# VectorE in traced order through the down-projection and final norm, with the row sums added on GpSimd

## The chip, the core and the metric

The kernel runs on one core of one Trainium2 chip. A core has five engines, each with an instruction queue of its own that it works through in order: TensorE (PE, matmuls; its weight loads are shown as PEld), VectorE (DVE), ScalarE (ACT), GpSimd (POOL) and SyncE (SP, which here only issues DMA transfers). Engines wait for each other through semaphores. Matmul results land in PSUM, eight banks of 128 x 512 numbers; everything else sits in SBUF, and the inputs, the output and the large intermediate arrays in HBM.

The metric is the device time of one execution in microseconds, less is better.

## The reference

One layer of a hybrid backbone over 2048 latent tokens of width 1024, with 256 context tokens. What matters here is its end: the gated MLP of 2816 channels, its down-projection with the residual, and the final norm.

```python
def rmsnorm(x, gain):
    xf = x.astype(jnp.float32)
    y = xf * lax.rsqrt(jnp.mean(xf * xf, axis=-1, keepdims=True) + EPS)
    return (y * gain.astype(jnp.float32)).astype(x.dtype)
...
    return (a * jax.nn.gelu(gc, approximate=False)) @ w_down
...
        x = x + g1 * (o @ w_out[l])
        h2 = modulate(rmsnorm(x, norm_ffn[l]), sh2, sc2)
        x = x + g2 * conv_ffn(h2, w_up[l], conv_w[l], conv_b[l], w_down[l], rows)
...
    return rmsnorm(x, norm_final)
```

Everything before it (condition vectors, the two mixers, the output projection, the up-projection and the convolution) is the same in both kernels.

## The kernel before

**Precision.** A product of two float32 matrices is made of three matmuls (`mm3`): each operand is split into a high part, which ACT casts (`split`, L120), and a low part, which DVE or POOL subtracts (L121); high x high, high x low and low x high are added up in PSUM.

**The stage.** The down-projection multiplies the activations `m` (2816 channels, kept in HBM as `m_d`) by `w_down` (`wd_d`). Rows and columns are halved, and instead of eight products of half matrices seven are made, from sums and differences of halves (Strassen's scheme). Product q (0 to 6) runs over eleven pieces j of the 2816 channels. So the stage has 77 steps, n = 11 q + j. A step is 24 matmuls: for each of eight 128-row chunks i, one `mm3` into bank i of PSUM. Steps 0 to 2 are prepared in the stage before; the last four, 73 to 76, are not done piece by piece but chunk by chunk at the very end, so that the chunks finish one after the other.

**What is done around a step.** The program traces, in this order, at step n: `load(n + 3)`, the DMA loads from HBM; `prepare(n + 2)`, the casts and sums for the step two later; the 24 matmuls; at j = 10 an eviction of each bank (`evict`, L1673 to L1677); and at other j one function from the list `side`. In detail:

- `load` gives a step its tiles: activations in `mr` (128 x 1024, four buffers), weights in `sT` (128 x 512; eleven places that stay and a ring of five that is reused), sums of activations in `sS`. All these loads go through `get` (L1540), which pins them to their traced order on SP's queue. A load into a buffer waits for the buffer's last reader.
- `prepare` in q = 4 first subtracts two activation tiles (L1586) and two weight tiles (L1587); then `cast` makes high and low parts: `mhl`, three slots used in turn (so the cast for step n + 2 waits for the end of step n - 1 on PE), and `th`, `tl`. In q = 1, 2, 3 and 5 it then updates the sums that later products use (L1591 to L1599; in q = 5 L1599, `sT` minus a freshly loaded weight tile).
- `evict` adds a finished bank to the row sums `odd` or `even` or copies it there. The next product's first matmul into that bank waits for it.
- `side` holds what is left over: adding `odd` to `even` (L1648 to L1652), then, in the steps of q = 5, finishing the odd rows' sums (L1656), adding the residual `xn` to them (`odd_rows`, L1619) with half of their sum of squares on ACT; and in the steps of q = 6, squares, root and scaling of the even rows (`row_out`, L1611).

**The tail.** After the last four steps of chunk i, `odd_sum(i)` subtracts the bank from the row (L1627) and lets ACT square and sum it (L1628); `odd_out(i - 1)` adds the two halves of the sum of squares of the row before on DVE (L1632), POOL makes the root in two instructions (`rstd`: multiply and add, L113; power of -1/2, L115), DVE scales the row (L1611) and SP stores it. The last row is scaled in two halves, by DVE (L1637) and ACT (L1639), and stored in two transfers (L1641).

**What sets the order.** The framework schedules the traced program: a planner plays it through with its own estimates of durations and puts an instruction on its engine's queue when, by these, it is ready, earlier traced ones first. So on each engine the order on the queue can differ from the traced one. `pin` (`keep_in_program_order`) keeps an instruction behind the one traced just before it on the same engine; it adds no wait. Pinned before are SP's loads through `get` and a few instructions of earlier stages. In the stage described here DVE, ACT, POOL and PE are all left to the planner.

Of the kernel before, what the change touches and what calls it, by code (L numbers as in the profile page):

```python
# [9 lines left out]
F32 = mybir.dt.float32  # L10
# [3 lines left out]
AF = mybir.ActivationFunctionType  # L14
ALU = mybir.AluOpType
# [3 lines left out]
P = 128  # L19
D = 1024  # L20
# [3 lines left out]
NCH = TH // P  # L24
# [7 lines left out]
EPS = 1e-6  # L32
# [21 lines left out]
class Tensor:  # L54
# [12 lines left out]
    def transpose(self, out, in_, identity):  # L67
        self.t += 0.109
        return self.engine.transpose(out, in_, identity)


@with_exitstack
def tile_trunk(ctx, tc, x, c, cx, c_ctx, w_ada, b_ada, norm_mix, norm_ffn, w_in, hg_norm, sgu_g, sgu_b,
               w_sp, b_sp, w_out, w_up, conv_w, conv_b, w_down, norm_final, masks, out):
    nc = tc.nc
    V, S, G, T = nc.vector, nc.scalar, nc.gpsimd, Tensor(nc.tensor)
    ld = nc.sync.dma_start
    st = nc.sync.dma_start
    pin = tc.keep_in_program_order
# [13 lines left out]
    mhalf = cst.tile([P, 8], F32, name="mhalf")  # L93
# [16 lines left out]
    def rstd(pool, ss, n, scale, bias=EPS, keep=lambda i: i, out=None):  # L110

        r = pool.tile([P, 8], F32, tag="rs", name="rs")
        keep(G.tensor_scalar(out=r[:, :n], in0=ss, scalar1=scale, scalar2=bias, op0=ALU.mult, op1=ALU.add))  # L113
        r2 = pool.tile([P, 8], F32, tag="rs2", name="rs2") if out is None else out
        G.tensor_tensor(out=r2[:, :n], in0=r[:, :n], in1=mhalf[:, :n], op=ALU.pow)  # L115
        return r2
# [12 lines left out]
    class Pump:  # L129
# [3 lines left out]
        def __init__(self):  # L133
            self.tasks, self.soon, self.at = [], [], 0.0
# [43 lines left out]
    with es1:  # L178
# [36 lines left out]
        def x_sums():  # L215
            return pm.tile([P, 8], F32, tag="xss", name="xss", bufs=2)
# [83 lines left out]
        with tc.manual_schedule():  # L300
# [19 lines left out]
            ss = x_sums()  # L320
# [10 lines left out]
            for k in range(NK):  # L331
                for i in range(2):
                    o = (k % 2) * 256 + i * P
# [17 lines left out]
            for w in range(2):  # L351
                for j in range(4):
                    o = 2 * (4 * w + j)
# [722 lines left out]
        i = len(seq) - 4  # L1076
# [31 lines left out]
    def dbank():  # L1108
        return ps2.tile([P, 2, 512], F32, tag="dn", name="dn", bufs=2)
# [14 lines left out]
    class Unit:  # L1124
# [11 lines left out]
        def load(self):  # L1136
            for k in range(2):
                self.load_half(k)
# [48 lines left out]
    with tc.tile_pool(name="po", bufs=1, reuse_waits="tile") as po:  # L1187
# [58 lines left out]
        for t, (hh, g) in enumerate(tiles):  # L1246
            if g % 2 == 0:
                ss = px.tile([P, 2], F32, tag="ss", name="ss", bufs=2)
# [9 lines left out]
            pd = dbank()  # L1258
            o = ops.pop(t)
# [189 lines left out]
    def down(pd, n, i, first, last):  # L1449
        mh, ml, wh, wl = ops[n]  # L1450
        sl = slice(i * P, (i + 1) * P)
        mm3(pd, mh[:, sl], ml[:, sl], wh, wl, first, last)
# [54 lines left out]


    ps3 = ctx.enter_context(tc.tile_pool(name="ps3", bufs=1, space=PSUM, reuse_waits="tile"))

    def banks():
        return [ps3.tile([P, 512], F32, tag="dn", name="dn", bufs=8) for i in range(NCH)]
# [6 lines left out]
    pd_ = ctx.enter_context(tc.tile_pool(name="pd", bufs=1, reuse_waits="tile"))  # L1519
    sT = pb.tile([P, NR * 4 * 512], F32, tag="xah", name="sT", align_bytes=AL)  # L1520
    sS = pd_.tile([P, NJ, TH], F32, tag="sS", name="sS", align_bytes=AL)
    odd = [pd_.tile([P, 2, 512], F32, name=f"odd{i}") for i in range(NCH)]
    even = [pd_.tile([P, 2, 512], F32, name=f"even{i}") for i in range(NCH)]
    nf = pd_.tile([P, D], F32, name="nf")
    nw = [0]
    ra, rb = {}, {}

    def mr():
        return pd_.tile([P, TH], F32, tag="mr", name="mr", bufs=4)
# [9 lines left out]
    def get(t, src):  # L1539
        pin(ld(t, src))  # L1540
        return t
# [37 lines left out]
    def prepare(n):  # L1579

        if n >= 7 * NJ:
            return
        q, j = divmod(n, NJ)
        (a, b), (a2_, b2) = ra.pop(n), rb.pop(n, (None, None))
        if q == 4:
            V.tensor_sub(a, a, a2_)  # L1586
            V.tensor_sub(b, b, b2)  # L1587
        cast(n, a, b, slot_s(n), slot_t(n))
        S_, T_ = sS[:, j, :], sTj(j)
        if q == 1:  # L1590
            V.tensor_add(S_, a2_, S_)  # L1591
            V.tensor_sub(T_, b2, T_)
        elif q == 2:
            V.tensor_sub(S_, S_, a2_)
            V.tensor_sub(T_, b2, T_)
        elif q == 3:
            V.tensor_sub(S_, a2_, S_)
        elif q == 5:
            V.tensor_sub(T_, T_, b2)  # L1599

    def square(t, ss):
        jk = pd_.tile([P, D], BF16, tag="jk", name="jk")
        S.activation(jk[:, :t.shape[-1]], t, AF.Square, accum_out=ss)  # L1603

    def flat(t):
        return t.rearrange("p a b -> p (a b)")

    def row_out(ti, t, ss):

        r = rstd(pd_, ss, 1, 1.0 / D)  # L1610
        V.scalar_tensor_tensor(out=t, in0=t, scalar=r[:, 0:1], in1=nf, op0=ALU.mult, op1=ALU.mult)  # L1611
        st(out[ti * P:(ti + 1) * P, :], t)

    xts, odd_ss = {}, {}

    def odd_rows(i):

        o = odd[i]
        V.tensor_add(flat(o), flat(o), xts.pop(i))  # L1619
        odd_ss[i] = pd_.tile([P, 2], F32, name=f"oss{i}")  # L1620
        square(o[:, 1, :], odd_ss[i][:, 1:2])
        if i == NCH - 1:
            V.tensor_mul(o[:, 1, :], o[:, 1, :], nf[:, 512:])

    def odd_sum(i, pd):
        o, ss = odd[i], odd_ss[i]
        V.tensor_sub(o[:, 0, :], o[:, 0, :], pd)  # L1627
        S.activation(pd, o[:, 0, :], AF.Square, accum_out=ss[:, 0:1])  # L1628

    def odd_out(i):  # L1630
        o, ss = odd[i], odd_ss[i]
        V.tensor_add(ss[:, 0:1], ss[:, 0:1], ss[:, 1:2])  # L1632
        if i < NCH - 1:
            row_out(NCH + i, flat(o), ss[:, 0:1])
            return
        r = rstd(pd_, ss[:, 0:1], 1, 1.0 / D)
        V.scalar_tensor_tensor(out=o[:, 0, :], in0=o[:, 0, :], scalar=r[:, 0:1], in1=nf[:, :512],  # L1637
                               op0=ALU.mult, op1=ALU.mult)
        S.mul(o[:, 1, :], o[:, 1, :], r[:, 0:1])  # L1639
        for n in (1, 0):  # L1640
            st(out[(NCH + i) * P:(NCH + i + 1) * P, n * 512:n * 512 + 512], o[:, n, :])  # L1641
# [3 lines left out]
    def sums_behind(q, i):  # L1645
        o, e = odd[i], even[i]
        if q == 1:
            side.append(lambda: V.tensor_add(e[:, 0, :], e[:, 0, :], o[:, 0, :]))  # L1648
        elif q == 3:
            def f():  # L1650
                V.tensor_add(e[:, 1, :], e[:, 1, :], o[:, 0, :])
                V.tensor_add(e[:, 1, :], e[:, 1, :], o[:, 1, :])  # L1652
            side.append(f)
        elif q == 4:
            def f():
                V.tensor_add(o[:, 1, :], o[:, 1, :], o[:, 0, :])  # L1656
                xts[i] = get(mr(), xn_d[NCH + i])
                if i > 1:
                    odd_rows(i - 2)
            side.append(f)  # L1660
            if i == NCH - 1:
                side.extend([lambda: odd_rows(i - 1), lambda: odd_rows(i)])
        elif q == 5:
            def f():
                ss = pd_.tile([P, 2], F32, tag="ss", name="ss", bufs=4)
                square(flat(e), ss[:, 0:1])
                row_out(i, flat(e), ss[:, 0:1])
            side.append(f)

    def evict(q, i, pd):  # L1670
        o, e = odd[i], even[i]
        if q in (0, 2):
            S.copy(o[:, q // 2, :], pd)  # L1673
        elif q in (1, 5):
            V.tensor_add(e[:, q // 5, :], pd, e[:, q // 5, :])
        elif q in (3, 4):
            V.tensor_add(o[:, 0, :], pd, o[:, 0, :])  # L1677
        sums_behind(q, i)
# [9 lines left out]
    for n in range(3, 7 * NJ - NB):  # L1688
        q, j = divmod(n, NJ)
        if j == 0:  # L1690
            pds = banks()
        if n in range(4, 4 + NCH):
            ld(flat(even[n - 4]), xn_d[n - 4])
        if n == 2 * NJ - 3:
            ld(nf, norm_final.rearrange("(o d) -> o d", o=1).broadcast_to([P, D]))
        if n == 6 * NJ:
            tail = pd_.tile([P, NJ * TH], F32R, tag="sS", name="tail", align_bytes=AL)
            tail_s = tail[:, :8 * TH].rearrange("p (s w c) -> p s w c", s=4, w=2)
        if q < 6:
            load(n + 3)  # L1700
            prepare(n + 2)
        else:
            for k in ((2,), (3,), (4,), (5,), (6, 7), (8, 9), (10,))[j]:
                prepare(6 * NJ + k)
            for k in ((3,), (4,), (5, 6), (7, 8), (9, 10), (), ())[j]:
                load(6 * NJ + k)
        for i in range(NCH):
            down(pds[i], n, i, j == 0, j == NJ - 1)
            if j == NJ - 1:
                evict(q, i, pds[i])  # L1710
        for _ in range(1 + (q == 6)):
            if side and j < NJ - 1:
                side.pop(0)()
    assert not side
    for i in range(NCH):
        for n in range(7 * NJ - NB, 7 * NJ):
            down(pds[i], n, i, False, n == 7 * NJ - 1)
        odd_sum(i, pds[i])
        if i:
            odd_out(i - 1)  # L1720
    odd_out(NCH - 1)


# [19 lines left out]
```

## Time and profile before

| | |
|---|---|
| median of 3 runs | 2509.79 us (2508.38 to 2512.24) |
| profiled execution | 2513.77 us, its span from first to last instruction 2511.9 us |
| busy in the span | PE 97%, PEld 80%, DVE 72%, POOL 42%, ACT 38% |
| first matmul of the stage | 2065.3 us |
| mean granted TensorE clock | 0.993 |

A row of the timeline gives start, duration, engine, line of the kernel, operation, tile written <- tiles read, shapes, and in brackets how long the engine was idle before and what ended that. A row of the waits gives who waited for whom, us in total, times, longest. `dn` is a PSUM bank; L65 is every matmul, L120 every cast, L121 every low part, as helpers have one line each. A duration on DVE or ACT includes a part that overlaps the next instruction: a 128 x 1024 row of 1.22 us is followed by the next after 1.14, a 128 x 512 row of 0.68 after 0.60.

### The profile page before, as it was taken

Reading aid. Unit: us, or ns where it says so; the run is one execution under the profiler, and the core shown is the slowest. Engines: PE = TensorE matmul, PEld = TensorE weight load, DVE = VectorE, ACT = ScalarE, POOL = GpSimd, SP = SyncE. Lnnn points to the kernel's source line nnn. Section 1 sums busy time; section 2 is a strip of 40 time slices with the busy share of each in tenths; the row PEclk is TensorE's granted clock in tenths of the full one; section 3 lists DMA queues with packets and bytes.
Section 4 is the critical chain, followed back from the end, with each engine's and each line's share of the span. In section 5 each row is a group of like instructions: output and inputs, shape, how many; then the busy total and the mean of one; then the engine's idle time right before and its main releaser. Section 6 shows DMA issues by size and latency. Waiting matters only on the chain.

```text
span 2511.9 us, 32816 instructions
## 1 busy us (share of the span) xinstructions
PE 2440.4 (97%) x11859; PEld 2015.6 (80%) x11859; DVE 1796.9 (72%) x2375; ACT 964.2 (38%) x1606; POOL 1062.2 (42%) x871
## 2 busy tenths in 40 slices
PE   7999999899999999999999999999999999999998
PEld 4787888788888888788788888878788888888786
DVE  5866875645766766465798877759999983767775
ACT  2554334433444443354443333333333333332252
POOL 1344232332343443100688788777777860000002
PEclk8999999999999999999999999999999999999999
DMA  8356446573354323768822222562222238835544
GB/s 293 97 185 189 133 128 193 175 250 126 106 176 143 118 97 104 257 211 255 298 86 80 88 88 87 176 227 83 84 90 92 91 122 341 298 118 182 182 151 172
DMA packets 307838, 400.13 MB, mean 159 GB/s; under 512 B 33105, under 2 KB 216137, under 8 KB 304605
## 3 DMA queue, kind: packets, MB, share of 16 engines
q1 hardware_dynamic: 304420, 397.30, 47.5%
q8 instruction: 94, 1.54, 0.3%
q10 hardware_dynamic: 3257, 0.75, 0.1%
q14 instruction: 67, 0.55, 0.1%
HBM read 288.85 MB, written 109.13 MB: 158 GB/s over the span
## 4 chain that ended last, share of the span: by engine, by line
PE 38%; DVE 7%; DMA 2%; POOL 2%; issue 2%; ACT 1%; SPq 0%; POOLq 0%; DVEq 0%; ACTq 0%
PE up L65 24%; PE dn L65 14%; DVE dn L1331 3%; DMA sT<-wd 1%; POOL Al L121 1%; DVE edges L1336 1%; DVE gp L1407 0%; DMA raw<-in_w_up_dram 0%; DVE mhl L121 0%; POOL raw L1158 0%; DMA yl<-yd 0%; DVE odd L1611 0%; POOL fl L1154 0%; DMA xn<-cv 0%; DVE tl L121 0%
## 5 line engine op out<-in xcount | busy, mean ns | idle before, releaser
L1331 DVE SCALAR_TENSOR_TENSOR dn<-gp,taps,dn 128x1024 f32<-128x1024 f32 x352 | 448.2, 1280 | 20.7 <-ACT dn L1328 17.4
L121 POOL TENSOR_TENSOR Al<-raw,Ah 128x512 fp32r<-128x512 f32 x264 | 344.9, 1313 | 99.7 <-ACT Ah L120 93.1
L65 PE MATMUL pj<-xh,whi 128*128 128x512 f32 x896 | 363.8, 406 | 0.5 <-ACT xh L120 0.5
L65 PE MATMUL dn<-th,mhl 128*128 128x512 f32 x1120 | 353.0, 396 | 5.2 <-DVE odd L1677 4.8
L65 PE MATMUL pj<-xl,whi 128*128 128x512 f32 x896 | 350.7, 392 | 1.8 <-DVE xl L121 1.1
L65 PE MATMUL pj<-xh,wlo 128*128 128x512 f32 x896 | 350.8, 391 | 1.0 <-DVE wlo L121 1.0
L65 PE MATMUL up<-xah,Ah 128*128 128x512 f32 x704 | 277.1, 394 | 1.7 <-ACT Ah L120 1.7
L65 PE MATMUL up<-xah,Al 128*128 128x512 f32 x704 | 276.4, 393 | 2.4 <-POOL Al L121 2.4
L65 PE MATMUL up<-yl,Ah 128*128 128x512 f32 x704 | 274.6, 390 | 2.1 <-DMA yl<-yd 2.1
L120 ACT CAST Ah<-raw 128x512 fp32r<-128x512 f32 x264 | 160.5, 618 | 295.3 <-PE up L65 238.8
L65 PEld LDWEIGHTS dn<-th,mhl 128*128 128x128 f32 x1120 | 212.0, 189 | 54.8 <-issue 4.6
L121 POOL TENSOR_TENSOR wlo<-raw,whi 128x1024 fp32r<-128x1024 f32 x56 | 136.8, 2442 | 250.3 <-ACT whi L120 228.2
L113 POOL TENSOR_SCALAR rs<-ss 128x2 f32<-128x2 f32 (+1 forms) x16 | 8.2, 512 | 535.4 <-ACT jk L1603 368.9
L65 PE MATMUL dn<-tl,mhl 128*128 128x512 f32 x560 | 220.9, 394 | 0.0
L65 PE MATMUL up<-yh,Ah 128*128 128x512 f32 x528 | 208.2, 395 | 0.0
L65 PE MATMUL up<-yh,Al 128*128 128x512 f32 x528 | 206.9, 392 | 0.0
L65 PE MATMUL up<-xal,Ah 128*128 128x512 f32 x528 | 205.6, 389 | 0.0
L65 PEld LDWEIGHTS pj<-xh,wlo 128*128 128x128 f32 x896 | 168.3, 188 | 37.2 <-DVE wlo L121 1.7
L65 PEld LDWEIGHTS pj<-xh,whi 128*128 128x128 f32 x896 | 168.8, 188 | 33.9 <-issue 3.5
L65 PEld LDWEIGHTS pj<-xl,whi 128*128 128x128 f32 x896 | 168.9, 188 | 32.9 <-DVE xl L121 2.1
L65 PE MATMUL dn<-wo,o 128*128 128x512 f32 x768 | 183.1, 394 | 1.5 <-DVE nt L673 0.9
L65 PEld LDWEIGHTS dn<-wo,o 128*128 128x128 f32 x768 | 141.9, 188 | 31.2 <-issue 1.1
(320 smaller groups left out, 4673.5 us busy)
## 6 DMA issues: line engine op xcount, KB each, us to landing
raw<-in_w_up_dram SPq DMA_DIRECT2D x88, 512.0 KB
mr<-m SPq DMA_DIRECT2D x85, 512.0 KB
raw<-in_w_in_dram SPq DMA_DIRECT2D x68, 512.0 KB
sT<-wd SPq DMA_DIRECT2D x88, 256.0 KB
raw<-in_w_ada_dram SPq DMA_DIRECT2D x32, 512.0 KB
m<-cv SPq DMA_DIRECT2D x22, 544.0 KB
raw<-in_w_down_dram SPq DMA_DIRECT2D x22, 512.0 KB
wd<-raw SPq DMA_DIRECT2D x22, 512.0 KB
```

The lines of the kernel that those rows point to most:

```text
L65: return self.engine.matmul(out, lhsT, rhs, **kw)
L113: keep(G.tensor_scalar(out=r[:, :n], in0=ss, scalar1=scale, scalar2=bias, op0=ALU.mult, op1=ALU.add))
L120: keep(S.copy(hi, raw))
L121: (eng or G).tensor_sub(lo, raw, hi.bitcast(F32))
L1331: V.scalar_tensor_tensor(out=cr, in0=gt[:, t // 3:t // 3 + RH, t % 3:t % 3 + GW], scalar=taps[:, t * NF + f:t * NF + f + 1], in1=cr, op0=A ...
L1336: V.scalar_tensor_tensor(out=e[:, 0, :], in0=gt[:, 1, t % 3:t % 3 + GW], scalar=taps[:, t * NF + f:t * NF + f + 1], in1=e[:, 0, :], op0=AL ...
```

## The change

From the start of the stage's own code (after the matmul banks `ps3` are set up) the name `V`, through which every DVE instruction is given, is a wrapper that pins each instruction. Functions defined earlier, `split` and `cast` among them, use the same name and are pinned too from then on. So all DVE instructions of the stage stay in traced order. ACT, POOL and PE stay with the planner, but for the square of `odd_sum`, which is pinned on ACT.

The root is computed anew: POOL adds to the sum of squares either the constant D x EPS or a second sum to which DVE has added that constant in `odd_rows`; the power follows as before, with four buffers instead of one. For the odd rows it is traced right behind the square (`odd_sum`), and DVE's one-column add of the two halves (L1632) is gone. As the root is now of the sum and not of the mean, the weights `nf` are multiplied by the square root of D once, on ACT, behind their load.

```diff
+class Kept:
+    def __init__(self, engine, pin):
+        self.engine, self.pin = engine, pin
+
+    def __getattr__(self, name):
+        f = getattr(self.engine, name)
+        return lambda *a, **kw: self.pin(f(*a, **kw))
...
     ps3 = ctx.enter_context(tc.tile_pool(name="ps3", bufs=1, space=PSUM, reuse_waits="tile"))
+    V = Kept(nc.vector, pin)
...
-    def row_out(ti, t, ss):
-        r = rstd(pd_, ss, 1, 1.0 / D)
+    def root(ss, plus=D * EPS):
+        a, r = (pd_.tile([P, 1], F32, tag=t, name=t, bufs=4) for t in ("ra", "rr"))
+        G.tensor_scalar(out=a, in0=ss, scalar1=plus, scalar2=None, op0=ALU.add)
+        G.tensor_tensor(out=r, in0=a, in1=mhalf[:, :1], op=ALU.pow)
+        return r
+
+    def row_out(ti, t, r):
         V.scalar_tensor_tensor(out=t, in0=t, scalar=r[:, 0:1], in1=nf, op0=ALU.mult, op1=ALU.mult)
...
         square(o[:, 1, :], odd_ss[i][:, 1:2])
+        V.tensor_scalar(out=odd_ss[i][:, 1:2], in0=odd_ss[i][:, 1:2], scalar1=D * EPS, scalar2=None, op0=ALU.add)
...
-        S.activation(pd, o[:, 0, :], AF.Square, accum_out=ss[:, 0:1])
+        pin(S.activation(pd, o[:, 0, :], AF.Square, accum_out=ss[:, 0:1]))
+        roots[i] = root(ss[:, 0:1], ss[:, 1:2])
...
-        o, ss = odd[i], odd_ss[i]
-        V.tensor_add(ss[:, 0:1], ss[:, 0:1], ss[:, 1:2])
+        o, r = odd[i], roots[i]
         if i < NCH - 1:
-            row_out(NCH + i, flat(o), ss[:, 0:1])
+            row_out(NCH + i, flat(o), r)
             return
-        r = rstd(pd_, ss[:, 0:1], 1, 1.0 / D)
...
-                row_out(i, flat(e), ss[:, 0:1])
+                row_out(i, flat(e), root(ss[:, 0:1]))
...
             ld(nf, norm_final.rearrange("(o d) -> o d", o=1).broadcast_to([P, D]))
+            S.mul(nf, nf, float(D) ** 0.5)
```

More of the change, by code (lines that the diff above doesn't have):

```diff
@@ L1621, in odd_rows @@
         square(o[:, 1, :], odd_ss[i][:, 1:2])
+        V.tensor_scalar(out=odd_ss[i][:, 1:2], in0=odd_ss[i][:, 1:2], scalar1=D * EPS, scalar2=None, op0=ALU.add)
         if i == NCH - 1:
             V.tensor_mul(o[:, 1, :], o[:, 1, :], nf[:, 512:])
+    roots = {}
     def odd_sum(i, pd):
```

## The prediction

> **What bounds the kernel now.** I read the page first: busy shares of the whole span.
>
> ```profile
> PE 2440.4 (97%) x11859; PEld 2015.6 (80%) x11859; DVE 1796.9 (72%) x2375; ACT 964.2 (38%) x1606; POOL 1062.2 (42%) x871
> ```
>
> TensorE (PE) is busy 97% of 2511.9 us, so a change to VectorE (DVE) can only give what PE waits, what PE runs slowly, and the tail after the last matmul. Next I read the waits of PE in the changed stage (2060 us to the end), the same for DVE, and stretches of that stage by window (columns: busy time and count of PE, PEld, DVE, ACT, POOL; granted clock; DMA share; GB/s). The last two rows are windows of PE alone.
>
> ```profile
> PE dn L65 <- DVE odd L1677: 4.8, 2, 4.2
> DVE sT L1599 <- DMA sT<-wd: 21.5, 9, 3.4
> ```
> ```profile
> 2081.00:2122.00 41.00, 41.00 (x181) 33.64 (x180) 11.07 (x13) 9.41 (x12) 0.00 (x0) 1.00 1.00 400
> 2369.00:2374.00 5.00, 0.82 (x4) 0.42 (x3) 1.79 (x3) 1.56 (x2) 0.00 (x0) 0.89 0.32 105
> 2374.00:2380.00 6.00, 5.38 (x13) 3.74 (x13) 6.00 (x10) 0.00 (x0) 0.00 (x0) 0.52 0.51 167
> ...
> 2250.00:2300.00 50.00, 50.00 (x220) 1.00 0.41 138
> 2400.00:2450.00 50.00, 50.00 (x216) 1.00 0.46 152
> ```
>
> The stage has one PE wait worth naming: 4.8 us for evictions (L1677), the longer part 4.2 us, and behind it the granted clock is 0.52 for 6 us. From about there on 50 us hold 216 matmuls instead of 220 at clock 1.00. The timeline says why the eviction was late:
>
> ```profile
> 2334.13 1.21 DVE L121 TENSOR_TENSOR mhl<-mr,mhl 128x1024 fp32r<-128x1024 f32 x1
> 2340.69 1.23 DVE L1586 TENSOR_TENSOR mr<-mr 128x1024 f32<-128x1024 f32 x1 [1.80 <-DMA mr<-m]
> 2341.83 1.22 DVE L121 TENSOR_TENSOR mhl<-mr,mhl 128x1024 fp32r<-128x1024 f32 x1
> ...
> 2363.78 1.05 ACT L120 CAST mhl<-sS 128x1024 fp32r<-128x1024 f32 x1 [4.02 <-PE dn L65]
> 2368.09 0.68 DVE L121 TENSOR_TENSOR tl<-sT,th 128x512 fp32r<-128x512 f32 x1
> 2369.07 0.40 PE L65 MATMUL dn<-th,mhl 128*128 128x512 f32 x1
> 2372.21 0.69 DVE L1599 TENSOR_TENSOR sT<-sT 128x512 f32<-128x512 f32 x1 [3.43 <-DMA sT<-wd]
> 2372.82 0.68 DVE L1677 TENSOR_TENSOR odd<-dn,odd 128x512 f32<-128x512 f32 x1
> 2373.65 0.77 PE L65 MATMUL dn<-th,mhl 128*128 128x512 f32 x1 [4.18 <-DVE odd L1677]
> 2379.47 0.78 PE L65 MATMUL dn<-th,mhl 128*128 128x512 f32 x2
> ```
>
> Counting the eleven L1599, the one at 2372.21 belongs to step 57; in the program it stands behind step 57's two low-part subtractions (L121), two steps later. The planner put it ahead of step 56's, and ahead of the evictions of step 54. Its operand comes into the ring slot that step 55's `tl` gave free (2368.09 + 0.68), landed 3.4 us later, and all of DVE stood still for it. The loop is visible before: the buffer freed by step 50's low part (ends 2335.34) is refilled and read by L1586 of step 52 at 2340.69, 5.35 us later, and only then comes step 51's low part at 2341.83: 7.7 us from one step's low part to the next. A step of PE takes 5.5 us (next fence: the cast that waits for PE's end of a step comes at 2285.61 and 2291.11). So DVE fell behind step by step until the evictions were late.
>
> ```profile
> 2285.61 1.05 ACT L120 CAST mhl<-sS 128x1024 fp32r<-128x1024 f32 x1 [3.92 <-PE dn L65]
> 2291.11 1.05 ACT L120 CAST mhl<-sS 128x1024 fp32r<-128x1024 f32 x1 [3.92 <-PE dn L65]
> ...
> 2390.04 1.22 DVE L121 TENSOR_TENSOR mhl<-sS,mhl 128x1024 fp32r<-128x1024 f32 x1
> 2391.18 0.69 DVE L121 TENSOR_TENSOR tl<-sT,th 128x512 fp32r<-128x512 f32 x1
> 2391.78 0.68 DVE L1656 TENSOR_TENSOR odd<-odd 128x512 f32<-128x512 f32 x1
> 2392.38 1.22 DVE L1619 TENSOR_TENSOR odd<-odd,mr 128x1024 f32<-128x1024 f32 x1
> 2393.52 1.29 DVE L1656 TENSOR_TENSOR odd<-odd 128x512 f32<-128x512 f32 x2
> ```
>
> The tail, last in time:
>
> ```profile
> 2480.39 0.39 PE L65 MATMUL dn<-th,tail 128*128 128x512 f32 x1
> 2480.82 0.69 DVE L1627 TENSOR_TENSOR odd<-odd,dn 128x512 f32<-128x512 f32 x1 [10.02 <-PE dn L65]
> 2499.81 0.40 PE L65 MATMUL dn<-th,tail 128*128 128x512 f32 x1
> 2504.03 0.68 DVE L1627 TENSOR_TENSOR odd<-odd,dn 128x512 f32<-128x512 f32 x1
> 2504.74 0.60 ACT L1628 ACTIVATE dn<-odd 128x512 f32<-128x512 f32 x1 [0.82 <-DVE odd L1627]
> 2505.13 1.28 DVE L1611 SCALAR_TENSOR_TENSOR odd<-odd,rs,nf 128x1024 f32<-128x1024 f32 x1 [0.42 <-POOL rs L115]
> 2505.27 0.19 ACT L1628 ACTIVATION_READ_ACCUMULATOR dn<-odd 128x1 f32 x1
> 2506.33 0.15 DVE L1632 TENSOR_TENSOR oss<-oss 128x1 f32<-128x1 f32 x1
> 2506.64 0.19 POOL L113 TENSOR_SCALAR rs<-oss 128x1 f32<-128x1 f32 x1 [1.55 <-DVE oss L1632]
> 2507.50 0.75 DVE L1637 SCALAR_TENSOR_TENSOR odd<-odd,rs,nf 128x512 f32<-128x512 f32 x1 [1.02 <-POOL rs L115]
> 2508.25 0.81 SPq L1641 DMA_DIRECT2D out_dram<-odd  x2
> ```
> ```profile
> 2435.64 0.19 ACT L1603 ACTIVATION_READ_ACCUMULATOR jk<-even 128x1 f32 x1
> 2435.98 0.44 POOL L113 TENSOR_SCALAR rs<-ss 128x1 f32<-128x1 f32 x1 [367.65 <-ACT jk L1603]
> ```
>
> PE ends at 2500.21, but the subtraction that reads its last bank starts at 2504.03: DVE went through chunk after chunk with subtraction, sum, scaling in a row, and is itself the bound there, 3.8 us behind PE.
>
> **The change, part by part.**
>
> *DVE order in steps 42 to 65.* It removes no work; it moves L1586, L1587 and L1599 behind everything traced earlier. I follow step 54 with its evictions. ACT's cast for step 56 is at 2363.78, so L121 for `mhl` runs from 1.1 us later for 1.14 (2390.04 to 2391.18), `tl` for 0.60, L1599 for 0.60: done 3.5 us after the end of step 53. The first eviction then ends at 4.1 us and each further one 0.6 us later; PE needs the first bank at 5.5 us and the others every 0.69 us (three matmuls). Nothing waits. The operand of that L1599 must have landed by then: its slot is freed by `tl` of step 54, two steps (11 us) earlier in the new order, and landings took 3.4 and 5.35 us. So 5.6 us are to spare. The loads keep their order on SP's queue and only start earlier, because they wait for DVE's reads. Steps 44 to 54 read 2 x 512 and 2 x 256 KB each, 1.5 MB in 5.5 us, 286 GB/s (an estimate); the window at 2081 us moved 400.
> Gain: from 2369.07 to 2379.47 PE starts 12 matmuls in 10.4 us, at 50/220 us each they take 2.73: **7.7 us**. Bounds: 0 (the wait stays) and 7.7; I take 7.7, since no row shows a second reason for the wait.
>
> *Spacing of matmuls.* 220 against 216 in 50 us is 4.2 ns each; 696 matmuls of steps 44 to 72 make 2.9 us. The change of spacing sits where PE's weight load first waited for a late eviction:
>
> ```profile
> 2307.62 2.48 DVE L1677 TENSOR_TENSOR odd<-dn,odd 128x512 f32<-128x512 f32 x4
> 2308.35 0.19 PEld L65 LDWEIGHTS dn<-th,mhl 128*128 128x128 f32 x1 [0.31 <-DVE odd L1677]
> ```
>
> Whether it goes with that wait no row shows. Bounds 0 and 2.9; between them I take half, **1.5 us**.
>
> *Tail.* In the traced order DVE does subtraction i+1 before the scaling of row i. Per chunk it needs 0.69 + 1.28 = 1.97 us, and PE takes (2499.81 - 2480.39)/7 = 2.77, so it keeps up. The last subtraction starts 0.04 after PE, 2500.25 (as at 2480.82); ACT 0.71 later (2504.03 to 2504.74); its sum is read 0.53 later for 0.19, 2501.68; POOL starts 0.15 after that (2435.64 + 0.19 to 2435.98), without DVE's add between; 0.86 later the last scaling, 2502.69, 0.75 long; the store at 2503.44 instead of 2508.25: **4.8 us**. Meanwhile DVE scales row 6 from 2500.94 to 2502.2, clear of 2502.69. POOL's add now takes a second operand from memory: bounds 0.15 (DVE's own add) and 0.44 (its longest row here) against 0.19, so -0.04 to +0.25; I take 0.19, the row with the same shape.
>
> The GPSIMD Engine Reference of the Trainium skill, section "Engine selection", says to keep elementwise work on VectorE, GpSimd being about twice as slow with two inputs. By that rule the add costs some 0.15 us more (an estimate) and the tail gives 4.65; by the rows the hop saved (2506.33 to 2506.64) is worth more than that.
>
> *New small work.* Eight one-column adds go to steps 55 to 64, each behind ACT's square of the row (0.53 + 0.19). A step there holds, in DVE's order, cast wait 1.1, L121 1.14 and 0.60, L1599 0.60, L1656 0.60, L1619 1.14, ACT's square about 0.8, the add 0.16: 6.1 us against 5.5. Behind the waiting add stands the next step's L121, and PE waits for that one two steps later. At worst each of ten steps lags 0.6, 6 us in all; a cast is done 2.9 us into its step and wanted at 11, so 8 us cover it: 0. Without that cover it would cost up to 6. The eight even rows (steps 66 to 69) wait for ACT and POOL as now, under the same 8 us. The multiplication of the weights is one ACT instruction of 1.05 us (as L120's, the same shape) near step 19, behind a load; ACT idles 3.92 us per step there, so 0, else 1.
>
> *Sum.* 7.7 + 1.5 + 4.8 = 14.0 us. The profiled execution took 2513.77 us (span 2511.9), so 2499.8 by it; the median of the runs, 2509.79, lies 4.0 lower, which gives **2495.8 us**, 0.6% faster. The 4 us may lie in the very waits that go, so the gain can be smaller by as much.
>
> **The rivals.**
> 1. *Only the tail gains.* The slots are too few and the loop stays whatever the order: five ring slots, two used per step. For it: nine waits of L1599 for its load. Against it: the loop closes only through an L1599 or L1586 that stands ahead of the previous step's L121. Time: 2509.8 - 4.8 = 2505.0. The Perfetto Trace Analysis page of the Trainium skill, section "Identifying the Most-Contended Engine", reads a repeating bubble as a sign of too few buffers; by it this rival would hold.
> 2. *It does not do what it says.* The planner could already have had DVE in traced order, or ACT's and SP's order, which stays its own, shifts and gives the gains back. Against the first half: row 2372.21 ahead of 2372.82. Time: 2509.8.
> 3. *Slower.* In order, DVE's waits for ACT in steps 55 to 65 become PE's. To decide, the lag per step must pass 0.8 us (8 us over ten steps), and 2.2 us to eat the 14 as well; that is a step of 7.7 us on DVE against my 6.1. It could come if ACT's squares are issued behind the next cast. With 2.8 per step, PE waits 20 us: 2509.8 - 14 + 20 = 2516.
>
> **How the numbers follow.** Chances: forecast 0.76, with its own range 2491 to 2500 (the spacing's bounds 2494.4 and 2497.3, the spread of the runs and the 4 us); rival 1, 0.10; rival 2, 0.06; rival 3, 0.08. The range of eight in ten reaches from 2491 to 2505 and leaves rivals 2 and 3 out. A measurement of this kernel tells 0.2%, 5 us, from no change. Faster: 0.76 and half of rival 1, 0.81; same: the other half and rival 2, 0.11; slower 0.08.
>
> **What would show it.** Right: PE waits for no eviction after 2300 us and the granted clock stays 1.00 until the end; L1599 waits for no load; in the tail the last subtraction starts within 0.1 us of the last matmul's end and the last store some 3.2 us after that end; matmuls at 220 in 50 us. Wrong: L1599 or L1586 still waiting for loads (rival 1); L121 waiting for ACT late in steps 57 to 66 and PE waiting for `mhl` or `tl` (rival 3).

## The result, and the profile after

The changed kernel takes 2497.79 us (median of 4 runs, 2495.68 to 2499.83) against 2511.01 us (2508.38 to 2513.20) for the kernel before, run beside it: a ratio of 0.9948, 95% interval 0.9933 to 0.9962, so 13.2 us less. 2495.8 was predicted. The profiled execution took 2497.09 us, its span 2495.3.

The waits of PE from 2060 us to the end have one row left, and the waits of DVE for weight tiles one, at 2135.66 us, far ahead of the steps in question:

```profile
PE dn L65 <- ACT th L131: 0.4, 1, 0.4
DVE sT L80 <- DMA sT<-wd: 0.7, 1, 0.7
```

In this kernel every DVE instruction of the stage stands under L80 (the wrapper), casts under L131. The rows of 4.8 us for evictions and of 21.5 us for loads are gone. The windows of PE alone (busy, matmuls, granted clock, DMA share, GB/s):

```profile
2300.00:2350.00 50.00, 50.00 (x221) 1.00 0.84 271
2400.00:2450.00 50.00, 50.00 (x220) 1.00 0.56 188
2374.00:2380.00 6.00, 6.00 (x28) 1.00 0.89 295
```

28 matmuls in the 6 us that held 13 before, clock 1.00, and 220 from 2400 to 2450 us where there had been 216. The next fence is the timeline of the evictions of step 54, and then the tail, from the root of the first odd row on:

```profile
2362.55 1.23 DVE L80 TENSOR_TENSOR mhl<-sS,mhl 128x1024 fp32r<-128x1024 f32 x1 [3.06 <-ACT mhl L131]
2363.70 0.68 DVE L80 TENSOR_TENSOR tl<-sT,th 128x512 fp32r<-128x512 f32 x1
2364.30 0.69 DVE L80 TENSOR_TENSOR sT<-sT 128x512 f32<-128x512 f32 x1
2364.90 4.87 DVE L80 TENSOR_TENSOR odd<-dn,odd 128x512 f32<-128x512 f32 x8
...
2470.32 0.30 POOL L1623 TENSOR_SCALAR ra<-oss 128x1 f32<-128x1 f32 x1 [30.08 <-ACT dn L1649]
...
2487.76 0.40 PE L65 MATMUL dn<-th,tail 128*128 128x512 f32 x1
2488.19 0.69 DVE L80 TENSOR_TENSOR odd<-odd,dn 128x512 f32<-128x512 f32 x1 [0.90 <-PE dn L65]
2488.79 1.28 DVE L80 SCALAR_TENSOR_TENSOR odd<-odd,rr,nf 128x1024 f32<-128x1024 f32 x1
2489.45 0.19 ACT L1649 ACTIVATION_READ_ACCUMULATOR dn<-odd 128x1 f32 x1
2489.73 0.50 POOL L1623 TENSOR_SCALAR ra<-oss 128x1 f32<-128x1 f32 x1 [1.62 <-ACT dn L1649]
2490.32 0.57 POOL L1624 TENSOR_TENSOR rr<-ra,mhalf 128x1 f32<-128x1 f32 x1
2490.93 0.75 DVE L80 SCALAR_TENSOR_TENSOR odd<-odd,rr,nf 128x512 f32<-128x512 f32 x1 [0.85 <-POOL rr L1624]
2491.67 0.81 SPq L1661 DMA_DIRECT2D out_dram<-odd  x2
```

The eight evictions run in one piece, without idle time: DVE starts them while PE still works on step 54 and finds each bank done when it comes to it. In the tail the last subtraction starts 0.03 us after PE's end (2487.76 + 0.40), and the store 3.51 us after it, where it had been 8.04.

For all that follows I split the stage of each profile in two: M, from the start of its first matmul to the start of its last, and T, from the end of the last matmul to the start of the last pair of stores. The first matmul of the stage came between 2061.0 and 2065.4 us in the fourteen profiles, for reasons that lie before it; M and T are free of that. After: M 423.60, T 3.51. Before (first profile): M 434.52, T 8.04. So the two profiles differ by 10.9 + 4.5 = 15.4 us in the stage, more than the 13.2 timed.

### The profile page after: what moved, and what is told of

It is laid out like the page before. It is cut to its first block, busy times and chain, and to the rows that moved or that the text cites. A ratio compares the mean times of both kernels' runs of the same rounds, so it can differ in the third digit from the quotient of the medians.

```text
span 2495.3 us, 32821 instructions
## 1 busy us (share of the span) xinstructions
PE 2435.9 (98%) x11859; PEld 2015.0 (81%) x11859; DVE 1796.6 (72%) x2375; ACT 964.7 (39%) x1607; POOL 1060.4 (42%) x871
## 4 chain that ended last, share of the span: by engine, by line
PE 44%; issue 2%; DVE 2%; POOL 2%; DMA 1%; ACT 0%; SPq 0%; POOLq 0%; ACTq 0%
PE up L65 30%; PE dn L65 14%; DVE dn L1342 1%; POOL Al L132 0%; DMA yl<-yd 0%; POOL ra L1623 0%; POOL rr L1624 0%; POOL raw L1169 0%; DMA xn<-cv 0%; DVE edges L1347 0%; DVE gp L1418 0%; POOL fl L1165 0%; DVE fl L132 0%; POOL cv L1429 0%; DVE fl L1218 0%
## 5 line engine op out<-in xcount | busy, mean ns | idle before, releaser
L65 PE MATMUL dn<-th,mhl 128*128 128x512 f32 x1120 | 346.9, 391 | 0.4 <-ACT th L131 0.4
L131 ACT CAST Ah<-raw 128x512 fp32r<-128x512 f32 x264 | 160.6, 618 | 294.0 <-PE up L65 232.8
L65 PEld LDWEIGHTS up<-yl,Ah 128*128 128x128 f32 x704 | 132.6, 188 | 33.7 <-DMA yl<-yd 4.4
```

The costliest lines, as they stand in the source:

```text
L65: return self.engine.matmul(out, lhsT, rhs, **kw)
L131: keep(S.copy(hi, raw))
```

## The experiments

Theory: an order in which the subtractions with loaded tiles (L1586, L1587, L1599) stand ahead of the previous step's low parts makes DVE late; with the order, wait, half clock and wider spacing go. The tail gains by order and new root together. Rivals: too few buffers; or one part of the change alone does it.

| kernel | M | T | stage against the mean of three profiles of before | timed ratio (95%) |
|---|---|---|---|---|
| before, three profiles | 434.52, 431.03, 430.72 | 8.04, 8.01, 8.02 | | second and third: one run each, 2508.37 and 2506.04 us |
| after | 423.60 | 3.51 | -13.0 | 0.9948 (0.9933 to 0.9962) |
| order only | 423.60 | 6.14 | -10.4 | 0.9966 (0.9956 to 0.9976) |
| root only | 432.23 | 9.96 | +2.1 | 1.0013 (1.0003 to 1.0023) |
| order up to step 72, root | 423.57 | 9.96 | -6.6 | 0.9981 (0.9972 to 0.9989) |
| order from step 73, root | 429.76 | 3.51 | -6.8 | 0.9988 (0.9979 to 0.9998) |
| three lines in order | 423.61 | 8.04 | -8.5 | 0.9970 (0.9958 to 0.9981) |
| three lines and evictions | 423.61 | 8.04 | -8.5 | 0.9964 (0.9953 to 0.9976) |
| ring of seven | 429.46 | 8.04 | -2.6 | 0.9995 (0.9984 to 1.0005) |
| after, evictions later | 424.24 | 3.52 | -12.4 | 0.9942 (0.9930 to 0.9954) |
| after, still later | 425.51 | 3.51 | -11.1 | one run, 2498.20 us |
| after, add of two tensors | 423.58 | 3.38 | -13.2 | 0.9931 (0.9909 to 0.9953) |

0.001 of the ratio is 2.5 us. But for the order kept from step 73, whose one profile caught a short M, each stage difference lies within its timed interval. The medians of order only (2500.42 us) and of the ring of seven (2509.67) lie above what was expected (2497.5 to 2499.5, and 2504 to 2508 by the theory).

**The kernel before, profiled twice more.** No edit.

> The kernel before, profiled once more. Theory (the loop's length is load time, so the wait differs from execution to execution): the order of VectorE is the same, first to last matmul of the stage differs from the 434.5 us of the first profile by more than 1 us, as 432.2 and 429.8 us differ between the two runs with the new root and this same order up to step 72. Rival (the wait is fixed by the order): 434.5 within 0.5 us.

> The same once more. Theory: again another value, between 429 and 435 us, and the wider spacing of the matmuls there in some executions and not in others. Rival: 434.5 within 0.5 us, and 216 matmuls in 50 us after 2308 us as in the first profile.

For the one and then for the other: the row of PE's waits for evictions, and windows of PE, one behind the first such wait and two around the later ones:

```profile
PE dn L65 <- DVE odd L1677: 3.6, 3, 1.3
```
```profile
2310.00:2360.00 50.00, 50.00 (x216) 1.00 0.71 229
2366.00:2372.00 6.00, 3.71 (x15) 1.00 0.25 87
2372.00:2378.00 6.00, 5.73 (x25) 1.00 0.49 175
```
```profile
PE dn L65 <- DVE odd L1677: 3.8, 2, 2.4
```
```profile
2310.00:2360.00 50.00, 50.00 (x220) 1.00 0.72 231
2366.00:2372.00 6.00, 3.60 (x9) 0.67 0.32 105
2372.00:2378.00 6.00, 6.00 (x22) 0.77 0.54 153
```

With one and the same order M was 434.5, 431.0 and 430.7, so the loss is not fixed by the order, as the theory said. But PE's waits for evictions differ little (4.8, 3.6 and 3.8 us); most of the difference is in what came behind them. The one profile had the wider spacing and no half clock, the other half clock and no wider spacing; the profile I had predicted from had both. (Why the clock fell in one and not in another is worked out in the last section.) That load times alone make the waits differ is argued, not shown. Against 423.6 the middle loses 10.9, 7.4 and 7.1 us, 8.5 in the mean, and with 4.5 of the tail that is 13.0, close to the 13.2 timed.

**The change in parts.** Order only: the wrapper, with the old sums and root. Root only: the new sums and root, without the wrapper. Then the whole change with the wrapper in one half of the stage:

```diff
 # order only, added to the kernel before
+    V = Kept(nc.vector, pin)
 # root only, taken from the changed kernel
-    V = Kept(nc.vector, pin)
 # order up to step 72: the changed kernel, ahead of the last four steps
+    V = nc.vector
 # order from step 73: the changed kernel, the wrapper set there instead
+    V = Kept(nc.vector, pin)
```

> The order of VectorE as in the changed kernel, sums and root as in the kernel before. Theory (order): the wait for the eviction, the half clock and the wider spacing all go with the order, 7.7 + about 2.9 us in the middle. In the tail VectorE then stands for GpSimd's root between a row's sum and its scaling, about 3.0 us per chunk against 2.77 of TensorE; last store 5 to 7 us after the last matmul's end (8.0 before, 3.5 after), so 1 to 3 us more. Sum: 11.5 to 13.5 us faster than before, 2497.5 to 2499.5. Rival (the gain of the middle is not the order's but comes with the new sums and root): wait of 4 us stays, time within 3 us of before.

> The new sums and root, VectorE's order left to the planner. Theory (order): the wait for the eviction of about 4 us and the half clock stay, 216 to 217 matmuls in 50 us behind them. The tail gets worse, since VectorE's queue then has each row's scaling ahead of the next subtraction and waits for ACT and GpSimd in every chunk: about 3.9 us per chunk against TensorE's 2.77, last store some 11.7 us after the last matmul's end (8.0 before). So 3 to 4 us slower than before, about 2514.5. Rival (the root alone gives the tail's gain): last store 3.5 to 5 us after the last matmul's end, 3 to 4.5 us faster, about 2506.5.

> The changed kernel, with VectorE's order given back to the planner for the last four steps chunk by chunk. Theory: the middle gains all of 7.7 + 2.9 = 10.6 us, the tail loses as in the root alone (store 11.7 us after the last matmul, 3.7 us worse than before): 7 us faster than before, about 2504. Rival (the order matters in the tail only): 2509 to 2514.

> The changed kernel, with VectorE's order given to the planner up to step 72 and kept only in the last four steps. Theory: the middle stays as before (wait of about 4 us for an eviction, half clock, 216 matmuls in 50 us), the tail gains 4.5 us (store 3.5 us after the last matmul): about 2506.5. Rival (the order matters in the tail only): 2497 to 2499.

The middle goes with the order alone: M is 423.6 in both kernels that keep it up to step 72, and 432.2 and 429.8 in the two that do not, near the 430.7 to 434.5 of the kernel before. Behind the waits of root only there are 220 matmuls in 50 us, not the 216 to 217 expected; with the order from step 73 the longest wait for an eviction was 1.3 us, not about 4. In the tail neither part does it alone. Two chunks of order only, then of root only:

```profile
2487.63 0.15 DVE L80 TENSOR_TENSOR oss<-oss 128x1 f32<-128x1 f32 x1
2488.80 1.29 DVE L80 SCALAR_TENSOR_TENSOR odd<-odd,rs,nf 128x1024 f32<-128x1024 f32 x1 [1.02 <-POOL rs L126]
...
2491.78 1.28 DVE L80 SCALAR_TENSOR_TENSOR odd<-odd,rs,nf 128x1024 f32<-128x1024 f32 x1 [1.02 <-POOL rs L126]
```
```profile
2496.45 0.30 POOL L1622 TENSOR_SCALAR ra<-oss 128x1 f32<-128x1 f32 x1 [2.77 <-ACT dn L1648]
2497.43 1.28 DVE L1628 SCALAR_TENSOR_TENSOR odd<-odd,rr,nf 128x1024 f32<-128x1024 f32 x1 [1.84 <-POOL rr L1623]
2498.63 0.68 DVE L1647 TENSOR_TENSOR odd<-odd,dn 128x512 f32<-128x512 f32 x1
...
2501.15 1.29 DVE L1628 SCALAR_TENSOR_TENSOR odd<-odd,rr,nf 128x1024 f32<-128x1024 f32 x1 [1.84 <-POOL rr L1623]
```

Order only: DVE adds the halves and stands 1.02 us for POOL, 2.98 us a chunk (2488.80 to 2491.78) against PE's 2.77; T 6.14, a gain of 1.9. Root only: the planner puts the scaling of a row right behind its subtraction, and DVE stands 1.84 us in each of its chunks of 3.72 (2497.43 to 2501.15); T 9.96, a loss of 1.9. I had expected 3.9 a chunk and T 11.7. Together they give 4.5.

**Which part of the order.**

```diff
-            V.tensor_sub(a, a, a2_)
-            V.tensor_sub(b, b, b2)
+            pin(V.tensor_sub(a, a, a2_))
+            pin(V.tensor_sub(b, b, b2))
...
-            V.tensor_sub(T_, T_, b2)
+            pin(V.tensor_sub(T_, T_, b2))
 # three lines and evictions: besides
-            V.tensor_add(e[:, q // 5, :], pd, e[:, q // 5, :])
+            pin(V.tensor_add(e[:, q // 5, :], pd, e[:, q // 5, :]))
-            V.tensor_add(o[:, 0, :], pd, o[:, 0, :])
+            pin(V.tensor_add(o[:, 0, :], pd, o[:, 0, :]))
```

> The kernel before, with only the three subtractions that wait for loads kept in traced order (two of activations and weights in q = 4, one of weights in q = 5). Theory (loop): those three standing ahead of the previous step's low parts are what makes VectorE fall behind, so the drift over steps 44 to 54 goes, and no row of these lines waits 2 to 3 us for its load again and again. But the planner still puts the low parts of step 57 and the subtraction ahead of the evictions of step 54: 1.1 + 0.6 + 0.6 us and the wait for the cast, so TensorE still waits once, 0.5 to 3 us, without 6 us of half clock. Time 4 to 8 us faster than before, 2502 to 2506. Rival (too few places in the ring): the nine waits for loads stay, the eviction's wait stays at about 4 us, time within 2 us of before. Spacing: if a wait for a late eviction sets it, 216 in 50 us remain from there on; if not, 220.

> The same three subtractions and VectorE's evictions kept in traced order, all else as before. Theory (order): no wait of TensorE for an eviction, clock 1.00, 220 matmuls in 50 us to the end, all 10.6 us of the middle; the tail as before (store 8.0 us after the last matmul). Time about 2500.5. Rival (the rest of VectorE's order counts too): waits of more than 1 us remain, time 2503 to 2508.

The timeline with the three lines alone in order:

```profile
2362.44 0.69 DVE L1677 TENSOR_TENSOR odd<-dn,odd 128x512 f32<-128x512 f32 x1 [2.84 <-PE dn L65]
2363.05 1.22 DVE L121 TENSOR_TENSOR mhl<-sS,mhl 128x1024 fp32r<-128x1024 f32 x1
2364.18 0.69 DVE L121 TENSOR_TENSOR tl<-sT,th 128x512 fp32r<-128x512 f32 x1
2364.78 0.68 DVE L1599 TENSOR_TENSOR sT<-sT 128x512 f32<-128x512 f32 x1
2365.39 4.27 DVE L1677 TENSOR_TENSOR odd<-dn,odd 128x512 f32<-128x512 f32 x7
```

Three lines give the whole gain of the middle: M 423.61, and 423.57 to 423.61 in all six profiles of kernels that keep them in order, the two with later evictions apart. I had expected the low parts of step 57 and its L1599 ahead of the evictions, and a wait of PE of 0.5 to 3 us; PE did not wait for an eviction at all. What stands ahead of seven of them is step 56's (ACT's cast for them starts at 2361.58, at the end of step 53), as in the traced order, where it stands ahead of all eight. DVE stood idle for 2.84 us until bank 0 was done, so it was no longer behind, and the 2.3 us in between do no harm. Keeping the evictions as well adds nothing: M is the same to 0.01 us, and the two timed ratios overlap.

**More buffers.** The kernel before with two more ring places (`more`):

```diff
+    more = pd_.tile([P, 2 * 512], F32, name="more")
...
-        o = NJ * 512 + (nw[0] - 1) % 5 * 512
+        k = (nw[0] - 1) % 7
+        if k > 4:
+            return more[:, (k - 5) * 512:(k - 4) * 512]
+        o = NJ * 512 + k * 512
```

> The kernel before with seven places in the ring of weight tiles instead of five, VectorE's order left to the planner. Rival 1 (too few buffers): the waits of the subtractions of weights for their loads go (before: nine, 21.5 us), the wait for the eviction shrinks to under 1 us, 7 to 10 us faster, 2500 to 2503. Theory (order): the loop over the activations' four buffers is left, and the planner still puts subtractions and low parts ahead of evictions, so the eviction's wait shrinks from 4.2 us but does not go; 2 to 6 us faster, 2504 to 2508.

The timeline, where L1599 is L1603 and the evictions L1681, and in a fence of its own the row of PE's waits for evictions:

```profile
2352.25 0.69 DVE L1603 TENSOR_TENSOR sT<-sT 128x512 f32<-128x512 f32 x1
2355.21 0.69 DVE L1603 TENSOR_TENSOR sT<-sT 128x512 f32<-128x512 f32 x1 [2.27 <-DMA sT<-wd]
2360.97 0.69 DVE L1603 TENSOR_TENSOR sT<-sT 128x512 f32<-128x512 f32 x1 [3.33 <-DMA sT<-wd]
2366.76 0.69 DVE L1603 TENSOR_TENSOR sT<-sT,more 128x512 f32<-128x512 f32 x1 [3.36 <-DMA more<-wd]
2367.36 0.68 DVE L1681 TENSOR_TENSOR odd<-dn,odd 128x512 f32<-128x512 f32 x1
```
```profile
PE dn L65 <- DVE odd L1681: 3.8, 2, 2.5
```

The rival falls: M 429.5, near the two lower profiles of before, and no difference in time that can be told. The 2 to 6 us that the theory had expected did not come either. Four L1599 now stand ahead of the first eviction of step 54 where there were three. The one at 2366.76 belongs to step 58: the planner used the places to put the subtraction one step further ahead, and the wait of 3.4 us came with it. More places for the activations, and more places with a fixed order, were not run.

**The spacing.** The changed kernel with two, then three multiplications on DVE ahead of the evictions of step 43; their results are not used:

```diff
+                if q == 3 and i == 0:
+                    for _ in range(2):   # then 3
+                        jd = pd_.tile([P, D], BF16, tag="jk", name="jd")
+                        V.tensor_mul(jd, nf, nf)
```

> The changed kernel with two multiplications of 128 x 1024 added on VectorE (results unused) ahead of step 43's evictions, so that TensorE waits once for a late eviction, some 0.4 us, early in step 44. Theory (the spacing is set by that wait): from there on 216 matmuls in 50 us, and about 2.9 us more by the end, with the wait 3 to 3.5 us slower than the changed kernel: 2501. Rival (the spacing has another cause): 220 in 50 us all through, 0 to 0.6 us slower, 2498.

> The changed kernel with three multiplications of 128 x 1024 added on VectorE (results unused) ahead of step 43's evictions, where two gave a wait of 0.4 us and left the spacing at 0.229 us. TensorE waits about 1.5 us. Theory (a longer wait for an eviction sets the wider spacing): 216 matmuls in 50 us from there on, first to last matmul 423.6 + 1.5 + 2.9 = 428 us. Rival (a wait alone does not set it): 220 in 50 us, 425.1 us.

With two, then with three, each the row of PE's waits and a window behind it:

```profile
PE dn L65 <- DVE odd L80: 0.4, 1, 0.4
```
```profile
2310.00:2360.00 50.00, 50.00 (x220) 1.00 0.79 252
```
```profile
PE dn L65 <- DVE odd L80: 1.7, 1, 1.7
```
```profile
2310.00:2360.00 50.00, 50.00 (x220) 1.00 0.74 237
```

A wait for an eviction at that place does not by itself set the wider spacing: M grew by 0.6 and 1.9 us, the waits and little else. Yet the spacing widened only behind such waits: near 2306 us in two of the three profiles of before and in the order kept from step 73 (where it went back at the next wait). In the first profile of before it also went back, at 2358.41, where a weight load waited 0.28 us for a low part, and came again behind the wait of 4.2 us. It never came in a kernel without such waits. What decides is open.

**The add on POOL.**

```diff
-        G.tensor_scalar(out=a, in0=ss, scalar1=plus, scalar2=None, op0=ALU.add)
+        if isinstance(plus, float):
+            G.tensor_scalar(out=a, in0=ss, scalar1=plus, scalar2=None, op0=ALU.add)
+        else:
+            G.tensor_tensor(out=a, in0=ss, in1=plus, op=ALU.add)
```

> The changed kernel, with GpSimd adding the two sums of a row as two tensors of one column instead of a tensor and a column operand. Theory (the column operand is what makes the add 0.50 us instead of the 0.19 of the row I took): the add takes about 0.19 to 0.3 us and the last store starts 3.2 to 3.3 us after the last matmul's end instead of 3.5; time the same within what can be told (0.3 us less). Rival (two operands cost 0.5 to 0.6 in either form, as the power with two tensors, 0.57): store 3.5 to 3.6 us after the last matmul's end.

The first of its adds, with DVE idle, and the last, beside DVE's scaling:

```profile
2471.56 0.19 POOL L1626 TENSOR_TENSOR ra<-oss 128x1 f32<-128x1 f32 x1 [30.06 <-ACT dn L1652]
...
2490.06 1.28 DVE L80 SCALAR_TENSOR_TENSOR odd<-odd,rr,nf 128x1024 f32<-128x1024 f32 x1
2490.97 0.41 POOL L1626 TENSOR_TENSOR ra<-oss 128x1 f32<-128x1 f32 x1 [1.73 <-ACT dn L1652]
```

Both theories had a part. The form costs 0.1 us (0.19 against 0.30 in the changed kernel at 2470.32, both alone). The other 0.2 comes from what DVE does meanwhile: 0.19 becomes 0.41 and 0.30 becomes 0.50 when the add starts inside a scaling of 1.28 us, and it ends just behind the scaling (at 2491.38 against 2491.34 here, at 2490.23 against 2490.07 in the changed kernel). In root only, where DVE waits for POOL, the add took 0.30. T is 3.38 instead of 3.51; no timing can tell that.

## Why the prediction was right, by its own steps

**DVE order, 7.7 us: right in mechanism, and right in size for the execution it was read from.** Evictions were to start 3.5 us after the end of step 53. The low part that starts 1.1 us after that end is at 2362.55, the evictions at 2364.90, 3.45 after it. No loaded tile was late in steps 42 to 65. For the loads I had estimated 286 GB/s; 271 ran over the window of 50 us above and 295 in that of 6 us. But 7.7 is one draw: the waits came to about 4 us in the second profile of before (7.4 less some 3 of spacing), without half clock, and waits and half clock to 7.1 in the third.

**Spacing, 1.5 us: the mis-sized term of the pair of profiles.** It gave the upper bound, 2.9: 220 matmuls in 50 us up to 2450. Over the three profiles of before it is about 3, 3 and 0, so 2 in the mean. The reason given, a wait for a late eviction, is not sufficient.

**Tail, 4.8 us: 4.5.** Subtraction, square and accumulator went as worked out, to 0.1 us. POOL's pair took 1.20 us (2489.73 to 2490.93) instead of 0.86. The step that failed is the price of the add: 0.19 "with the same shape" and an upper bound of 0.25 more, where 0.31 more was measured. I had called 0.44 its longest row, and the timeline of the kernel before has longer ones in the even rows:

```profile
2444.23 1.28 DVE L1611 SCALAR_TENSOR_TENSOR even<-even,rs,nf 128x1024 f32<-128x1024 f32 x1 [0.74 <-POOL rs L115]
2444.28 1.28 POOL L113 TENSOR_SCALAR rs<-ss 128x1 f32<-128x1 f32 x1
...
2504.27 0.19 POOL L113 TENSOR_SCALAR rs<-oss 128x1 f32<-128x1 f32 x1 [3.02 <-DVE oss L1632]
```

A one-column instruction of 0.19 us that starts just after a scaling has started lasts as long as the scaling; beside the subtraction of a bank (2504.03) it stays at 0.19. I had seen to it that the scaling of row 6 is clear of the last scaling, not that it is clear of POOL.

The SBUF — State Buffer page of the Trainium skill, section "Who interferes with whom", says that a VectorE instruction with two SBUF inputs contends with a GpSimd instruction that reads SBUF, and one with at most one SBUF input, outside the two-port modes, does not. The traces agree: the scaling reads row and weights from SBUF and POOL waits, the subtraction reads one of its two from PSUM and POOL does not. The rule of the GPSIMD Engine Reference of the Trainium skill, section "Engine selection", by which I weighed an add 0.15 us dearer and a tail of 4.65, comes nearer to the 4.5 measured than the row I took. That is luck: the add of two tensors, run alone on POOL, took 0.19 us against 0.15 on DVE, which is not twice as long.

**New small work, 0: right.** M is the same, to 0.04 us, with the one-column adds and without them (three lines in order). They do wait for ACT, nine microseconds in all, one of them here, and PE does not wait behind them:

```profile
2390.64 0.15 DVE L80 TENSOR_SCALAR oss<-oss 128x1 f32<-128x1 f32 x1 [1.54 <-ACT jk L1615]
```

**The sum** was 14.0; 15.4 by the two profiles, 13.0 by the mean of three profiles of before, 13.2 timed. The two errors, spacing and add, have opposite signs, and the first profile of before was a long one, as its 4.0 us over the median had hinted. That the sum came within 1 us of the gain is in part luck: waits and half clock were about 8, 4 and 7 us in the three profiles, and 7.7 was read from the dearest. The time forecast, 2495.8, was 2.0 us low: 0.8 of it in the gain, 1.2 because the kernel before took 2511.01 in the later runs and not 2509.79.

**The rivals.** "Only the tail gains" falls: order alone takes the middle's loss away, and two more ring places do not. The Perfetto Trace Analysis page of the Trainium skill, section "Optimization Strategy" (the prediction named the section just ahead of it), says that the same gap repeating on the engine that should be saturated can mean too few buffers. Here the repeating gaps were on DVE, while PE is the engine to keep busy, and with the buffers as they were the order took them away. "It does not do what it says" falls with M at 423.60. "Slower" falls with PE's single wait of 0.4 us.

## What to carry to other kernels

On an engine that works in order, an instruction that waits for a load and stands ahead of the one that frees the load's buffer makes a loop as long as the load (here up to 7.7 us a step against PE's 5.5); put it behind that reader before adding buffers, for a planner that orders by readiness may spend them on going further ahead. Price a small instruction by rows taken beside the same neighbours, not by its fastest row. And one profile is one draw: the same program lost 10.9, 7.4 and 7.1 us here, mostly by what its waits set off. Profile the kernel before more than once, and compare from the stage's first matmul.

## What the runs showed of the hardware

- Up to step 72 the same matmuls come every 0.229 us or every 0.233 us for stretches of tens to hundreds of us at full granted clock, and change at a wait. (Counts of a window take in matmuls that reach over its edges, hence 220 and 216 in 50 us.) In the third profile of before and with the later evictions, waits of 0.4 to 2.4 us left 220 in 50 us; in the first two profiles of before 216 followed on one. The cause is open.
- Half clock does not follow from every gap of this size: the second profile of before had waits of 1.2 and 1.3 us within 4 us and kept 1.00 (15 and 25 matmuls in 6 us each), the third had 2.4 and 1.3 us and fell to 0.67 and 0.77 (9 and 22). With the order kept from step 73, 1.0 and 1.3 us were enough for 0.50 from 2371.13 to 2374.54.
- The traces show what tells them apart. In each profile, from 100 us on, the times at which the granted clock changes are whole multiples of 3.413 us apart, so it goes by fixed stretches of that length. In the stretch just ahead of a fall in these steps PE was busy for 0.00 us (first profile of before), 0.94 (root only), 0.97 (third profile), 1.10 (ring of seven) and 1.14 (order from step 73). In the second profile of before the least was 1.94, and behind the later evictions 2.23, and the clock stayed 1.00. Over all fourteen profiles PE was busy for at most 1.98 us ahead of a fall, and for at least 1.50 in a stretch behind which the clock did not fall, so the limit lies between, near half (the ends of matmuls are modelled). The same gaps cost a half clock or not by how they fall against these stretches.
- A one-column add on POOL takes 0.19 or 0.30 us by its form, and 0.41 or 0.50 when it starts while DVE scales a row. An instruction of 0.19 that starts just after a scaling has started takes 1.28.
